# Norm stores moved to GpSimd's queue, and the first token half's transposed tiles copied to SBUF before they are split

## The chip, the cores and the metric

The kernel runs on one core of one Trainium2 chip. The metric is the device time of one execution in microseconds; lower is better. Before the change the median of three runs is 2728.11 us (2725.67, 2728.11 and 2728.45).

## What is computed

Two layers of a causal decoder on a sequence of 1024 tokens of width 1024, all in fp32. Layer 0 mixes tokens with dilated sliding-window attention, layer 1 with a gated linear recurrence (HGRN2). After each mixer comes a dense MLP, and every sub-layer ends in a layer norm:

```python
for i in range(DEPTH):                      # DEPTH = 2
    if i % 2 == 0:
        y = dilated_attention_mixer(x, attn_w_in[j], attn_w_out[j])
    else:
        y = hgrn2_mixer(x, hgrn_w_in[j], hgrn_w_out[j], hgrn_norm_g[j], lbs[i])
    x = layer_norm(ALPHA * x + y, ln_mix_g[i], ln_mix_b[i])
    y = jnp.square(jax.nn.relu(x @ ffn_w_up[i])) @ ffn_w_down[i]
    x = layer_norm(ALPHA * x + y, ln_ffn_g[i], ln_ffn_b[i])
```

The change touches the place, once per layer, where the mixer's output projection and its norm hand over to the MLP's up-projection.

## The kernel before, in words

**Numbers as pairs.** Every fp32 operand of a large matmul is split in two tiles: a high part (ScalarE copies it, rounded to `float32r`) and a low part (VectorE subtracts the high part from the source). A product is three matmuls: high by high, high by low, low by high. In the up-projection these are L1349, L1350 and L1351, of 128x128 weights by 512 columns; the low part of a weight tile `H` is needed first by L1351.

**Fast products.** The MLP uses a Strassen-like scheme with seven products on halves. The class `Fast` (L278 on) holds the normed input as transposed tiles: "11" and "21" for the first half of the tokens (tiles 0 to 3 of 128 tokens), "22" and "T1" to "T4" for the second half and for sums and differences of both.

**The norm stage, `outproj_ln` (L1062 on).** A closure `fin(t)` (L1187) finishes token tile `t`: the rows' remaining matmuls (L204 to L206) in one of three PSUM banks, the residual added by VectorE (L1199, L1201), the norm (`ln_math`, L214 on: statistics L228, scaling L230 and L244 on VectorE, small steps on ScalarE), and a store of 512 KB of the normed tile `z` to DRAM (L1204). The MLP's residual reads it back much later (L1516). `tr(t)` calls `Fast.add`, whose `z_tr` has TensorE transpose the tile (L253, four transposes to a bank) in the two PSUM banks of tag `pt`. In layer 0 the program's order is fin 0 to 3 with the column halves of tiles 5 and 6 in between, then tr 0, the rest of fin 6, tr 1, tr 2, the first half of fin 7, `weights()`, tr 3, fin 4, the second half of fin 7. `weights()` is the start of `ffn`: it asks for four 512 KB weight tiles `wa` (L1280) and splits the first three into `H` (L1310 on ScalarE, L1318 on VectorE). In layer 1 the order is similar, but fin 4 comes early and all of fin 7, both column halves, comes last.

**What `Fast.add` does with a tile of the first half.** `z_tr` leaves two banks `p0` and `p1`. For each of them `put` makes high and low parts in two steps of 256 columns (L263 on ScalarE, L264 on VectorE), both read from PSUM. Then both banks are copied whole to SBUF (`keep`, L321 and L322), for the sums of the second half. Only after that copy is a bank free for the next transposes. Tiles of the second half are transposed during the first up-products (`late`); GpSimd makes some of their differences (L328, L334).

**What sets the order.** All loads and stores touched here are issued by SyncE, whose queue (SPq) is in order: an issue that waits holds up those behind it. The instructions of an engine are put in an order when the program is built, by a planner that walks an estimated timeline, prefers what stands earlier in the program, and hands out buffers as it goes. Where the kernel wants an order of its own it pins it (`in_order`): for SyncE at the start of `outproj_ln`, and for TensorE, VectorE and SyncE from the seventeenth up-product on. The stage in between is left to the planner. Most SBUF tiles are slots of 4 KB per partition in one pool of 49 (`U`), and a slot is used again when its last reader, a store included, is done.

Of the kernel before, what the change touches and what calls it, by code (L numbers as in the profile page):

```python
# [12 lines left out]
AF = mybir.ActivationFunctionType  # L13
# [3 lines left out]
P = 128  # L17
# [52 lines left out]
def trunk_kernel(  # L70
# [24 lines left out]
    nc = tc.nc  # L95
# [10 lines left out]
    def bank(tag, name):  # L106
        return ps.tile([P, 512], F32, name=name, tag=tag, bufs={"mm": 3, "s": 2, "pt": 2, "o": 1}[tag])
# [4 lines left out]
    act = nc.scalar.activation  # L112
# [84 lines left out]
    def rows(ps_t, a, w, t, dm, ks, start, stop):  # L197

        n = len(ks)
        for i, k in enumerate(ks):  # L200
            ah, al = a[k]
            wh, wl = w[k][:2]
            c = slice(dm * 512, dm * 512 + 512)
            nc.tensor.matmul(ps_t, ah(t), wh[:, c], start=start and i == 0, stop=False)  # L204
            nc.tensor.matmul(ps_t, ah(t), wl[:, c], start=False, stop=False)
            nc.tensor.matmul(ps_t, al(t), wh[:, c], start=False, stop=stop and i == n - 1)  # L206
# [39 lines left out]
    def z_tr(z):  # L246

        out_ = []
        for j in range(2):
            pt = bank("pt", "lnpt")  # L250
            for i in range(4):
                k = j * 4 + i
                nc.tensor.transpose(pt[:, i * P:(i + 1) * P], z[:, k * P:(k + 1) * P], ident)  # L253
            out_.append(pt)
        return out_

    def put(his, los, src, c, eng=None):

        src = src.rearrange("p (k c) -> p k c", c=P)
        for i in range(2):  # L260
            hi = his[i].rearrange("p (k c) -> p k c", c=512)[:, :, c]
            lo = los[i].rearrange("p (k c) -> p k c", c=512)[:, :, c]
            act(hi, src[:, 2 * i:2 * i + 2], AF.Copy)  # L263
            (eng or nc.vector).tensor_sub(lo, src[:, 2 * i:2 * i + 2], hi.bitcast(F32))  # L264
# [13 lines left out]
    class Fast:  # L278
# [22 lines left out]
        def add(self, t, z):  # L301
            half, c = t // 4, slice((t % 4) * P, (t % 4) * P + P)
            first = not self.seen or self.seen[0] == half
            self.seen.append(half)
            v, g = nc.vector, nc.gpsimd
            p0, p1 = z_tr(z)

            def scratch(n):
                return wp.tile([P, 512], F32, name=f"fs{n}", tag="p" if n % 2 else "pts", bufs=3 if n % 2 else 4)

            def put_(n, src, eng=None):
                put(*self.tiles(n), src, c, eng)

            if half == 0:
                put_("11", p0)
                put_("21", p1)
            else:
                put_("22", p1)
            if first:
                a, b = ("11", "21") if half == 0 else ("12", "22")  # L320
                act(self.keep(a, t), p0, AF.Copy)  # L321
                act(self.keep(b, t), p1, AF.Copy)  # L322
                return
            t1, t2, t3, t4 = (scratch(n) for n in (1, 2, 3, 4))
            if half == 1:
                w12 = scratch(0)
                act(w12, p0, AF.Copy)
                g.tensor_sub(t1, w12, self.keep("11", t))  # L328
                v.tensor_sub(t3, p1, w12)
                v.tensor_sub(t2, p1, t1)  # L330
                yield
                put_("T2", t2)
                put_("T1", t1)
                g.tensor_sub(t4, self.keep("21", t), t2)  # L334
                yield
                put_("T3", t3)
                put_("T4", t4)
                return
            b22 = self.keep("22", t)
            v.tensor_sub(t1, self.keep("12", t), p0)  # L340
            g.tensor_sub(t3, b22, self.keep("12", t))
            g.tensor_sub(t2, b22, t1)
            put_("T1", t1)
            v.tensor_sub(t4, p1, t2)
            put_("T3", t3)
            yield
            put_("T2", t2)
            put_("T4", t4)
# [713 lines left out]
    def outproj_ln(pr, oN, fill, resid, gB_ap, bB_ap, keep, weights):  # L1062
# [15 lines left out]
        z = []  # L1078

        def load_z(t):  # L1080
            while len(z) <= min(t, 7):
                zt = U("z")
                nc.sync.dma_start(zt, resid(len(z)))
                z.append(zt)
# [102 lines left out]
        def fin(t, dms=(0, 1)):  # L1187
            load_z(t)
            for dm in dms:
                c = slice(dm * 512, dm * 512 + 512)  # L1190
                old = parts.get((t, dm), [])
                o = begun.pop((t, dm), None)
                fresh = o is not None or not old
                first = o is None
                if first:
                    o = bank("mm", "pmm")
                rows(o, a, w, t, dm, [k for k in range(NK) if k not in old], first, True)
                if fresh:
                    nc.vector.scalar_tensor_tensor(z[t][:, c], z[t][:, c], ALPHA, o, op0=ALU.mult, op1=ALU.add)  # L1199
                else:  # L1200
                    nc.vector.tensor_add(z[t][:, c], o, z[t][:, c])  # L1201
            if 1 in dms:
                ln_math(z[t], gB, bB, sums=pr.mixer == 0 and t in NSUM)
                nc.sync.dma_start(keep[t * P:(t + 1) * P, :], z[t])  # L1204

        if pr.mixer == 0:
            begin(5, 0, ks)
            begin(5, 1, ks, "s")
            fin(0)
            fin(5, (0,))  # L1210
            fin(1)
            fin(5, (1,))
            fin(2)
# [821 lines left out]
```

## Time and profile before

| | |
|---|---|
| median of 3 runs | 2728.11 us |
| the profiled execution | 2729.02 us, of which 2727.2 us is the span of the profile |
| granted TensorE clock, mean | 0.998 |
| the norm stage of layer 0, stores of `z` | from 1002.8 to 1040.5 us |
| the norm stage of layer 1, stores of `z` | from 2059.0 to 2110.9 us |
| issued by SyncE and ScalarE / by GpSimd | all DMAs / none |

How to read it: times in the trace count from the span's start. A busy TensorE is not TensorE at its peak: matmuls overlap, one of 512 columns is recorded with about 390 ns but the next starts about 227 ns after it. So the distance between starts tells a stall, and an idle time of zero does not rule one out.

### The profile page before, as it was taken

Reading aid. Unit: us, or ns where it says so; the run is one execution under the profiler, and the core shown is the slowest. Engines: PE = TensorE matmul, PEld = TensorE weight load, DVE = VectorE, ACT = ScalarE, POOL = GpSimd, SP = SyncE. Lnnn points to the kernel's source line nnn. Section 1 sums busy time; section 2 is a strip of 40 time slices with the busy share of each in tenths; the row PEclk is TensorE's granted clock in tenths of the full one; section 3 lists DMA queues with packets and bytes.
Section 4 is the critical chain, followed back from the end, with each engine's and each line's share of the span. In section 5 each row is a group of like instructions: output and inputs, shape, how many; then the busy total and the mean of one; then the engine's idle time right before and its main releaser. Section 6 shows DMA issues by size and latency. Waiting matters only on the chain.

```text
span 2727.2 us, 44137 instructions
## 1 busy us (share of the span) xinstructions
PE 2698.6 (99%) x16256; PEld 2199.0 (81%) x16256; DVE 2043.0 (75%) x3887; ACT 1387.0 (51%) x3044; POOL 28.3 (1%) x28
## 2 busy tenths in 40 slices
PE   9999999999999999999999999999999999999998
PEld 7787888888788677888888888788888888888887
DVE  8868877787787788776686686556578886678687
ACT  5555555555565456444554345556452544545443
POOL 0000000000000001000000000000000100000000
PEclk9999999999999999999999999999999999999999
DMA  7867666766867424553675652010242464485653
GB/s 297 273 225 236 210 219 204 239 224 213 257 209 237 126 105 171 186 200 137 220 253 180 221 170 93 32 62 32 74 128 110 150 224 166 152 305 176 221 177 127
DMA packets 208152, 493.66 MB, mean 181 GB/s; under 512 B 30016, under 2 KB 44864, under 8 KB 207936
## 3 DMA queue, kind: packets, MB, share of 16 engines
q1 hardware_dynamic: 206688, 489.53, 53.7%
q8 instruction: 128, 2.10, 0.3%
q10 hardware_dynamic: 1248, 1.31, 0.2%
q14 instruction: 88, 0.72, 0.1%
HBM read 362.69 MB, written 94.11 MB: 167 GB/s over the span
## 4 chain that ended last, share of the span: by engine, by line
PE 90%; DVE 6%; ACT 1%; DMA 1%; issue 1%; SPq 0%; DVEq 0%; ACTq 0%
PE pup L1351 7%; PE pup L1349 7%; PE pmm L828 7%; PE pup L1350 7%; PE pmm L826 7%; PE pmm L827 7%; PE pdy L1504 4%; PE pdy L1503 4%; PE pdy L1500 4%; PE pmm L192 3%; PE pdx L1503 3%; PE pdx L1504 3%; PE pdx L1500 3%; PE pmm L194 3%; PE pmm L193 3%; PE pmm L204 2%
## 5 line engine op out<-in xcount | busy, mean ns | idle before, releaser
L826 PE MATMUL pmm<-xh,H 128*128 128x512 f32 x1008 | 403.7, 400 | 1.6 <-ACT H L493 1.0
L828 PE MATMUL pmm<-xh,H 128*128 128x512 f32 x1008 | 395.0, 392 | 3.1 <-DVE H L501 2.9
L827 PE MATMUL pmm<-xl,H 128*128 128x512 f32 x1008 | 393.0, 390 | 0.9 <-DVE xl L158 0.9
L828 PEld LDWEIGHTS pmm<-xh,H 128*128 128x128 f32 x1008 | 189.2, 188 | 47.8 <-DVE H L501 6.9
L826 PEld LDWEIGHTS pmm<-xh,H 128*128 128x128 f32 x1008 | 189.5, 188 | 40.2 <-ACT H L493 1.9
L827 PEld LDWEIGHTS pmm<-xl,H 128*128 128x128 f32 x1008 | 189.7, 188 | 38.2 <-DVE xl L158 1.6
L1500 PE MATMUL pdy<-dT,dS 128*128 128x512 f32 x512 | 199.2, 389 | 0.0
L1503 PE MATMUL pdy<-dT,dS 128*128 128x512 f32 x512 | 199.2, 389 | 0.0
L1504 PE MATMUL pdy<-dT,dS 128*128 128x512 f32 x512 | 199.2, 389 | 0.0
L157 ACT ACTIVATE dS<-dr 128x512 fp32r<-128x512 f32 x192 | 119.4, 622 | 68.0 <-PE pdy L1504 36.2
L192 PE MATMUL pmm<-f0nh,wh 128*128 128x512 f32 x384 | 153.3, 399 | 0.0
L193 PE MATMUL pmm<-f0nl,wh 128*128 128x512 f32 x384 | 149.8, 390 | 0.0
L194 PE MATMUL pmm<-f0nh,wl 128*128 128x512 f32 x384 | 149.8, 390 | 0.0
L589 ACT ACTIVATE p<-p,stats 128x192 f32<-128x192 f32 (+1 forms) x256 | 108.9, 428 | 62.0 <-DVE stats L586 61.8
L158 DVE TENSOR_TENSOR dS<-dr,dS 128x512 fp32r<-128x512 f32 x192 | 130.9, 682 | 9.3 <-ACT dS L157 9.3
L157 ACT ACTIVATE dT<-hold 128x512 fp32r<-128x512 f32 x128 | 80.1, 625 | 80.3 <-DVE hold L1479 33.3
L1310 ACT ACTIVATE H<-wc 128x512 fp32r<-128x512 f32 x128 | 77.2, 625 | 78.4 <-DVE wc L1303 44.8
L1503 PEld LDWEIGHTS pdy<-dT,dS 128*128 128x128 f32 x512 | 96.1, 188 | 20.1
L1500 PEld LDWEIGHTS pdy<-dT,dS 128*128 128x128 f32 x512 | 96.1, 188 | 19.9
L1504 PEld LDWEIGHTS pdy<-dT,dS 128*128 128x128 f32 x512 | 96.1, 188 | 19.9
L586 DVE CUSTOM_DVE_ANT_0 p<-s,mask 128x192 f32<-128x192 f32 (+1 forms) x256 | 71.1, 337 | 45.6 <-PE s L573 32.6
L493 ACT ACTIVATE H<-wc 128x512 fp32r<-128x512 f32 x108 | 66.6, 629 | 75.3 <-DVE wc L485 73.3
(424 smaller groups left out, 6875.4 us busy)
## 6 DMA issues: line engine op xcount, KB each, us to landing
xh<-xtd SPq DMA_DIRECT2D x110, 512.0 KB
xl<-xtd SPq DMA_DIRECT2D x110, 512.0 KB
dr<-hd SPq DMA_DIRECT2D x192, 256.0 KB
dr<-in_w_down_dram SPq DMA_DIRECT2D x128, 256.0 KB
rot<-e SPq DMA_DIRECT2D x192, 128.0 KB
wa<-in_w_up_dram SPq DMA_DIRECT2D x48, 512.0 KB
wb<-in_w_attn_dram SPq DMA_DIRECT2D x36, 512.0 KB
wa<-in_w_attn_dram SPq DMA_DIRECT2D x33, 512.0 KB
```

What stands on the lines that cost most here:

```text
L157: act(hi, raw, AF.Copy)
L192: nc.tensor.matmul(o, wh[:, k], xs.h(k), start=k == 0, stop=False)
L193: nc.tensor.matmul(o, wh[:, k], xs.l(k), start=False, stop=False)
L194: nc.tensor.matmul(o, wl[:, k], xs.h(k), start=False, stop=k == NK - 1)
L826: nc.tensor.matmul(o, wh, hi[k // 2][:, c], start=begin and k == 0, stop=False, skip_group_check=True)
L827: nc.tensor.matmul(o, wh, lo[k // 2][:, c], start=False, stop=False, skip_group_check=True)
L828: nc.tensor.matmul(o, wl, hi[k // 2][:, c], start=False, stop=end and k == 3, skip_group_check=True)
L1349: nc.tensor.matmul(o, wh, xf.h(b, k), start=begin and k == 0, stop=False, skip_group_check=True)
L1350: nc.tensor.matmul(o, wh, xf.l(b, k), start=False, stop=False, skip_group_check=True)
L1500: nc.tensor.matmul(o[q], h, T_[:, L], start=begin, stop=False, skip_group_check=True)
L1503: nc.tensor.matmul(o[q], h, T_[:, R], start=False, stop=False, skip_group_check=True)
L1504: nc.tensor.matmul(o[q], l, T_[:, L], start=False, stop=end, skip_group_check=True)
```

## The change

Two edits. The first is in `Fast.add`: for a tile of the first half both banks are first copied whole to SBUF, and the four high and four low parts are then made from these copies and not from PSUM. The number of instructions and their sizes are the same. The second is in `fin`: the store of the normed tile is issued by GpSimd's queue instead of SyncE's. It applies to 16 stores, eight in each layer. The norms' stores inside `ffn` (L1536, L242) stay where they were.

```diff
@@ class Fast, add()
+            if first and half == 0:
+                for n, p in (("11", p0), ("21", p1)):
+                    act(self.keep(n, t), p, AF.Copy)
+                for n in ("11", "21"):
+                    put_(n, self.keep(n, t))
+                return
             if half == 0:
                 put_("11", p0)
                 put_("21", p1)
@@ outproj_ln, fin()
                 ln_math(z[t], gB, bB, sums=pr.mixer == 0 and t in NSUM)
-                nc.sync.dma_start(keep[t * P:(t + 1) * P, :], z[t])
+                nc.gpsimd.dma_start(keep[t * P:(t + 1) * P, :], z[t])
```

## The prediction

> **What bounds the kernel now.** I read the page first: busy times and the chain that ended last.
>
> ```profile
> span 2727.2 us, 44137 instructions
> PE 2698.6 (99%) x16256; PEld 2199.0 (81%) x16256; DVE 2043.0 (75%) x3887; ACT 1387.0 (51%) x3044; POOL 28.3 (1%) x28
> PE 90%; DVE 6%; ACT 1%; DMA 1%; issue 1%; SPq 0%; DVEq 0%; ACTq 0%
> ```
>
> TensorE sets the time. The change touches no matmul, so it can only win where TensorE stands still or runs at a lower clock, or lose by a new wait. Next, the busy times by stretches: the first five run through the hand-over of layer 0, the last lies in that of layer 1.
>
> ```profile
> 1030.00:1041.30 11.30, 8.30 (x29) 5.45 (x28) 10.32 (x20) 4.87 (x11) 1.27 (x1) 0.70 0.66 247
> 1041.30:1052.00 10.70, 10.70 (x52) 8.86 (x50) 7.48 (x11) 6.88 (x16) 3.10 (x2) 1.00 0.34 123
> 1052.00:1063.00 11.00, 9.64 (x44) 7.71 (x43) 10.92 (x24) 8.71 (x22) 2.81 (x1) 1.00 0.48 168
> 1063.00:1074.00 11.00, 11.00 (x55) 9.14 (x54) 8.90 (x18) 7.48 (x19) 2.65 (x2) 1.00 0.53 192
> 1074.00:1085.00 11.00, 10.91 (x52) 8.75 (x51) 11.00 (x21) 7.31 (x18) 3.61 (x2) 1.00 0.32 109
> 2090.00:2100.00 10.00, 10.00 (x51) 8.01 (x50) 7.15 (x15) 6.37 (x16) 0.00 (x0) 1.00 0.94 351
> ```
>
> Columns: length, then PE, PEld, DVE, ACT, POOL busy, the granted clock, DMA share, GB/s. Only 1030 to 1041.3 has a hole: TensorE is busy for 8.30 of 11.30 us, with a mean clock of 0.70, while VectorE is nearly full (10.32). The stretch of layer 1 has no hole and full clock: nothing is to be won there. TensorE in the hole, by its timeline:
>
> ```profile
> 1028.80 1.04 PE L253 MATMUL lnpt<-ident,z 128*128 128x128 f32 x8
> 1029.90 0.40 PE L206 MATMUL pmm<-woh,aol 128*128 128x512 f32 x1
> 1031.84 1.15 PE L253 MATMUL lnpt<-ident,z 128*128 128x128 f32 x8 [1.53 <-ACT af11r L321]
> 1033.18 0.85 PE L253 MATMUL lnpt<-ident,z 128*128 128x128 f32 x4 [0.20 <-ACT fs L327]
> 1033.70 0.80 PE L1349 MATMUL pup<-af11h,H 128*128 128x512 f32 x1
> 1037.40 0.80 PE L1351 MATMUL pup<-af11h,H 128*128 128x512 f32 x1 [1.26 <-DVE H L1318]
> 1038.00 0.63 PE L1349 MATMUL pup<-af11h,H 128*128 128x512 f32 x1
> 1038.43 0.63 PE L1350 MATMUL pup<-af11l,H 128*128 128x512 f32 x1
> 1040.46 0.40 PE L1349 MATMUL pup<-af11h,H 128*128 128x512 f32 x1
> 1040.69 0.39 PE L1350 MATMUL pup<-af11l,H 128*128 128x512 f32 x1
> 1041.38 0.39 PE L1349 MATMUL pup<-af11h,H 128*128 128x512 f32 x1
> ```
>
> The last row matmul ends at 1029.90 + 0.40 = 1030.30. Then TensorE waits 1.53 us for a bank that tile 3 still holds (L321 copies it to SBUF last), 0.20 us for the copy L327, and from 1033.70 for the up-projection's weights: it gets the first few matmuls done and stands until the low half of `H` is there (1037.40). Starts there are 0.43 us apart (1038.00 to 1038.43), from 1040.46 on 0.23: that is the half clock behind the 0.70. Without any of it, 12 transposes at 1.04/8 = 0.13 us at most and the 15 up-matmuls before 1041.38 at 0.23 us would end at 1030.30 + 1.56 + 3.45 = 1035.3. So **the hole is worth 6.1 us, and no more**.
>
> **The change part by part: stores.** SyncE's queue and the engines that feed the hole:
>
> ```profile
> 1002.77 23.93 SPq L1204 DMA_DIRECT2D x1d<-z  x6
> 1026.74 0.42 SPq L1083 DMA_DIRECT2D z<-in_x_dram  x1
> 1027.26 2.53 SPq L1280 DMA_DIRECT2D wa<-in_w_up_dram  x4
> 1032.82 8.03 SPq L1204 DMA_DIRECT2D x1d<-z  x2
> 1029.43 0.38 ACT L263 ACTIVATE af11h<-lnpt 128x256 fp32r<-128x256 f32 x1 [0.62 <-PE lnpt L253]
> 1031.18 0.60 ACT L321 ACTIVATE af11r<-lnpt 128x512 f32<-128x512 f32 x1
> 1031.68 0.59 ACT L322 ACTIVATE af21r<-lnpt 128x512 f32<-128x512 f32 x1
> 1032.53 0.60 ACT L327 ACTIVATE fs<-lnpt 128x512 f32<-128x512 f32 x1 [0.26 <-PE lnpt L253]
> 1033.02 0.62 ACT L1310 ACTIVATE H<-wa 128x512 fp32r<-128x512 f32 x1
> 1034.24 1.15 ACT L1310 ACTIVATE H<-wa 128x512 fp32r<-128x512 f32 x2 [0.59 <-DMA wa<-in_w_up_dram]
> 1031.52 1.27 DVE L244 SCALAR_TENSOR_TENSOR z<-z,lnw,bB 128x1024 f32<-128x1024 f32 x1
> 1033.91 1.28 DVE L228 BATCH_NORM_STATS2 lnst<-z 128x6 f32<-128x512 f32 x2
> 1035.46 1.28 DVE L230 SCALAR_TENSOR_TENSOR z<-z,lnmv,gB 128x1024 f32<-128x1024 f32 x1
> 1036.66 1.89 DVE L1318 TENSOR_TENSOR H<-wa,H 128x512 fp32r<-128x512 f32 x3
> 2114.80 0.73 ACT L263 ACTIVATE hfT2h<-fs 128x256 fp32r<-128x256 f32 x2
> ```
>
> Six stores stand ahead of the tile-7 load and the four weight loads on SyncE, and each waits for its norm: the weights are asked for at 1027.26 and the last split in this stretch still waits for one at 1034.24. Moved away, the stores hold up no load; the loads then go when their slots are free, at the earliest after the last issue before the stores and at the latest at 1027.26, so they gain between 0 and 24 us of lead (1026.74 - 1002.77). I take a few us, since the planner hands slots out in program order, behind those of tile 2's copies. On GpSimd's queue the same stores still wait for their norms. Behind them stand only L328 and L334:
>
> ```profile
> 1033.21 1.27 POOL L328 TENSOR_TENSOR fs<-fs,af11r 128x512 f32<-128x512 f32 x1 [939.20 <-ACT fs L327]
> 1047.94 1.67 POOL L334 TENSOR_TENSOR fs<-af21r,fs 128x512 f32<-128x512 f32 x1 [13.46 <-DVE fs L330]
> 1048.38 1.51 DVE L264 TENSOR_TENSOR afT2l<-fs,afT2h 128x256 fp32r<-128x256 f32 x1
> L264 DVE TENSOR_TENSOR af11l<-lnpt,af11h x8: 409/424/425, 1013.4 to 1030.7; 128x256 fp32r<-128x256 f32 x8
> L1516 SPq DMA_DIRECT2D z<-x1d x8: 319/350/424, 1444.4 to 1489.7; - x8
> ```
>
> Had the first L328 to wait for the last store (1032.82 + 8.03 = 1040.85), it would end at 1042.1 and still be ahead of the chain that takes it (13.46 us idle before L334). No row shows an issue by GpSimd: I bound it by SyncE's 2.53/4 = 0.63 us and GpSimd's own 1.67 us per instruction. 16 of them are 10 to 27 us on an engine that is busy for 28.3 of 2727.2 us; on TensorE's path I take 0, as the stored rows are first read at 1444.4 (L1516) and until then only the slots of `z` wait for a landing (rival 3).
>
> **Copies first.** Tile 3's first bank is full at 1029.43. Before, four split steps alternate between ScalarE and VectorE for 1031.18 - 1029.43 = 1.75 us and then come the copies. After, the copies run at 1029.43 and 0.50 us later (spacing of L321 and L322), so the banks are free at 1030.03 and 1030.53, when TensorE wants them at 1030.30 and 0.5 us later: **the 1.53 us wait goes**. The price: the splits end later. From SBUF, ScalarE's high parts follow each other without waiting for VectorE (2114.80: two in 0.73 us), so four take some 1.25 us behind the copies, to 1030.43 + 1.25 = 1031.7 instead of 1031.2. Next late is L327: behind the splits it runs 1031.7 to 1032.3 and not to 1033.13, so the third group of transposes still waits, and the first split of `H` ends at 1032.8 instead of 1033.65. Of the 1.53 us some 0.85 stay as gain at the first up-matmul.
>
> **The low half of `H`** ends last: 1037.40. VectorE has no idle time ahead of it; L1318 stands behind tile 7's statistics and scaling because the planner expected the weights late. With the loads ahead, and tile 2's and 3's copies 1.75 us earlier, it should expect them some 2 to 3 us earlier. Then L1318 goes ahead of L228, L229 and L230 and starts at about 1033.9 instead of 1036.66: 2.75 us. VectorE's splits of tile 3 start about 1 us later than now, which I charge with 0.55 us on that chain. So L1351 starts at 1037.40 - 2.75 + 0.55 = 1035.2.
>
> **The clock.** Here the half clock began in a pause of 1033.70 - 1030.30 = 3.40 us in which TensorE ran only transposes. That pause shrinks to about 2.5 us, and I take it that the clock stays full. From L1351 to 1041.38 are 11 matmuls; at 0.23 us they end at 1035.2 + 2.5 = 1037.7: **3.7 us gained**. With half clock as now (3.98 us from L1351 to 1041.38) it is 2.2 us; I take 3.7, since the pause is shorter than the only one that halved the clock here. [...]
>
> **Is it given back?** VectorE's idle time from 1041.3 to 1085 is 3.22 + 0.08 + 2.10 + 0 = 5.4 us, so it can follow 3.7 us, with little left; TensorE is full behind the hole, so the gain should last to the end.
>
> [...] Before, L264 reads one operand from PSUM; now both come from SBUF. Beside GpSimd's L334 a step with both from SBUF took 1.51 us (1048.38), those from PSUM at most 0.425 us. L328 at 1033.21 moves with L327 to about 1032.4 and the last splits end near 1032.1, so I take 0; caught, one step costs 1.51 - 0.42 = 1.1 us on VectorE's chain. [...]
>
> **Sum.** 2729.02 - 3.7 = 2725.3 for the profiled execution, which lies 0.9 us above the median: **2724.4 us**. Differences within 0.2% (5.5 us) can hardly be told from none.
>
> **The rivals.**
> (1) All of the hole goes: the loads, issued early, let the planner put L1310 and L1318 ahead of tile 3. For it: SyncE issues nothing but stores from 1002.77 to 1026.70, so the loads have 24 us to be early. Against: slots. 2728.11 - 6.1 = 2722.0.
> (2) VectorE holds it: L1318 stays behind tile 7's norm. For it: VectorE's chain has no gap from 1031.52 to 1036.66, and the splits of tile 3 come later. Then L1351 starts at 1037.4 to 1038.0, up to 1039.1 if GpSimd's read costs 1.1 us: nothing gained, up to 1.7 us lost. 2728 to 2730; also the case in which the change does not do what it says, since the bank was not what came last.
> (3) Slower: slots. Before tile 0 is transposed, 41 of 49 slots hold output weights, projections, seven `z` and the norm's factors; with twelve for the new tiles, eight freed, `z` 7, four `wa` and three `H` it is 53, so four of the last take over slots of `z` 0 to 3, whose stores now go another way. If a store is late by GpSimd's queue, `H` waits. For a loss of 5.5 us the first up-matmul must slip from 1033.70 to 1039.2, so tile 3's store, issued by 1026.7, must take 12 us to land. Against: 512 KB at the 247 GB/s of that stretch take 2.1 us. About 2734, the half clock included.
>
> **How the numbers follow.** Forecast 0.47, rival 1 0.18, rival 2 0.21, rival 3 0.14. Faster by over 0.2%: most of rival 1 and a quarter of the forecast, where the pause or L1318 comes out better, 0.28. Slower by over 0.2%: 0.13, rival 3. Within: 0.59. The range takes rival 1 less the 2.4 us by which the lowest run lies under the median, and reaches above rival 2 towards rival 3: 2719.6 to 2731.5.
>
> **What would show it.** In the profile after, the weights' issue moves ahead of 1027 and SyncE no longer waits on `z`; the wait on L321 is gone; L1318 starts near 1034; the clock of this stretch is near 1.00 and not 0.70; layer 1 is unchanged. If L1318 still starts at 1036 or later, rival 2 is right. If `H` or `wa` waits for a store's landing, rival 3. A new idle time of TensorE in layer 1 would make the whole sum wrong.

## The result and the profile after

The change makes the kernel a little faster: the median is 2723.65 us (20 executions, 2721.81 to 2725.72) against 2727.87 us before (20 executions, 2725.24 to 2729.61). The ratio is 0.9986, with a 95% interval of 0.9979 to 0.9992; that is 4.2 us, or 0.15%. The forecast was 2724.4 us. The profiled execution took 2721.81 us, of which 2720.0 us is its span.

The page after, with the span, the busy times and the chain that ended last:

```profile
span 2720.0 us, 44143 instructions
PE 2694.8 (99%) x16256; PEld 2199.3 (81%) x16256; DVE 2042.1 (75%) x3887; ACT 1385.0 (51%) x3044; POOL 39.2 (1%) x44
PE 92%; DVE 5%; ACT 1%; issue 1%; DMA 0%; POOL 0%; SPq 0%; DVEq 0%; ACTq 0%; POOLq 0%
```

GpSimd has 16 more instructions, the stores' issues, and is busy for 10.9 us more (39.2 against 28.3). VectorE's share of the chain falls from 6% to 5%. The same stretches as before, by windows (length, then PE, PEld, DVE, ACT, POOL busy, clock, DMA share, GB/s):

```profile
1030.00:1041.30 11.30, 11.30 (x56) 9.41 (x55) 11.17 (x22) 5.59 (x14) 2.80 (x3) 1.00 0.12 49
1041.30:1052.00 10.70, 7.78 (x42) 6.14 (x41) 10.70 (x21) 7.54 (x20) 4.55 (x3) 1.00 0.67 245
```

The hole is gone: from 1030 to 1041.3 TensorE is busy throughout and the clock is 1.00 instead of 0.70. But a new, smaller hole has opened behind it: in the next stretch TensorE is busy for 7.78 of 10.70 us, where it had been full before, and VectorE for 10.70 of 10.70 us, where it had 3.22 us to spare. TensorE by its timeline after:

```profile
996.45 0.39 PE L206 MATMUL pmm<-woh,aol 128*128 128x512 f32 x1
1028.27 0.39 PE L206 MATMUL pmm<-woh,aol 128*128 128x512 f32 x1
1028.50 0.39 PE L1355 MATMUL pup<-af11h,H 128*128 128x512 f32 x1
1033.94 1.04 PE L253 MATMUL lnpt<-ident,z 128*128 128x128 f32 x8
1037.59 0.39 PE L1355 MATMUL pup<-af21h,H 128*128 128x512 f32 x1
1046.21 0.50 PE L1357 MATMUL pup<-af11h,H 128*128 128x512 f32 x1 [1.68 <-DVE H L1324]
1050.45 0.63 PE L253 MATMUL lnpt<-ident,z 128*128 128x128 f32 x4 [1.24 <-DVE fs L336]
1104.35 0.39 PE L1355 MATMUL pup<-af22h,H 128*128 128x512 f32 x1
```

(Line numbers behind L311 are 6 higher after: L1318 is now L1324, L1349 to L1351 are L1355 to L1357.) The first up-matmul, 1028.50, follows the last row matmul, 1028.27, at full pace. Tile 3's transposes are done by then, and the first of the second half's tiles is transposed only at 1033.94, after two products. Then come the new stalls: 1.68 us for a low part of `H`, 1.24 us for a bank that VectorE's L336 still reads.

What this is worth is read from matmuls that both kernels have: the 261st row matmul (L204 to L206), the start of the fourth up-product and that of the 26th. Before, they stand here:

```profile
997.46 0.39 PE L206 MATMUL pmm<-woh,aol 128*128 128x512 f32 x1
1046.13 0.39 PE L1349 MATMUL pup<-af21h,H 128*128 128x512 f32 x1
1110.35 0.39 PE L1349 MATMUL pup<-af22h,H 128*128 128x512 f32 x1
```

From the first to the second it is 48.67 us before and 41.14 after: **7.5 us gained**. From the first to the third it is 112.89 and 107.90: 5.0 us are left. So 2.5 us were given back, 0.5 of them four transposes that the changed kernel makes only behind the fourth product. Between the fourth and the seventh product it loses 3.0 us: the two stalls above (2.9 us) and eleven transposes more in that stretch (16 against 5), less a stall of 1.36 us that the kernel before has there, at 1056.40. Where the weights' loads, the low parts of their splits and the neighbours stand after:

```profile
992.44 33.64 SPq L1286 DMA_DIRECT2D wa<-in_w_up_dram  x5
1025.84 1.89 DVE L1324 TENSOR_TENSOR H<-wa,H 128x512 fp32r<-128x512 f32 x3
1034.49 1.27 DVE L230 SCALAR_TENSOR_TENSOR z<-z,lnmv,gB 128x1024 f32<-128x1024 f32 x1
1041.60 1.67 POOL L340 TENSOR_TENSOR fs<-af21r,fs 128x512 f32<-128x512 f32 x1 [0.32 <-DVE fs L336]
1042.03 1.52 DVE L264 TENSOR_TENSOR afT2l<-fs,afT2h 128x256 fp32r<-128x256 f32 x1
1044.34 1.26 POOL L334 TENSOR_TENSOR fs<-fs,af11r 128x512 f32<-128x512 f32 x1 [1.08 <-DMA hd<-upa]
1044.41 1.75 DVE L1324 TENSOR_TENSOR H<-wa,H 128x512 fp32r<-128x512 f32 x1
```

The loads start at 992.44 and not at 1027.26; the low parts are made at 1025.84, ahead of tile 3 and of the last scaling of the stage (L230 at 1034.49), where before they stood behind it (1036.66 behind 1035.46). In the give-back two of VectorE's steps are stretched beside a subtraction of GpSimd: L264 takes 1.52 us, L1324 1.75, where the same steps without it take 0.41 (1047.69) and 0.68 (1047.09). The kernel before has the same pair (L264 for 1.51 us at 1048.38, and the row below), in a stretch where VectorE is busy for only 7.48 of 10.70 us. So the stretching is not new; the full VectorE around it is.

```profile
1049.82 1.78 DVE L1318 TENSOR_TENSOR H<-wa,H 128x512 fp32r<-128x512 f32 x1
```

The two spans differ by 7.2 us and the medians by 4.2. About 1.0 us of that lies ahead of the 261st row matmul, and 1.2 us around a wait for ScalarE near 1168 us (0.68 us of idle time at 1168.31), which the changed kernel's profile lacks. That is not the change's doing, since a second profile of the same kernel (`a2_again`) has it like the kernel before (0.63 us at 1163.69). In that second profile the gain up to the 26th product is again 5.0 us. A single pair of profiles is good to 1 or 2 us here, not better.

Part of the 7.5 us is the half clock, which the profile before has from 1033.50 to 1040.33 and the profile after has nowhere in this stage. The gain in the median is not that half clock alone. Of the executions measured together with `a2_again`, those of the kernel before with a mean clock of 0.999 have a median of 2727.55 us (11 executions), those of the changed kernel with 0.999 have 2723.41 us (9).

### The profile page after: what moved, and what is told of

It reads as the page before. It is cut to its first block, busy times and chain, and to the rows that moved or that the text cites. A ratio compares the mean times of both kernels' runs of the same rounds, so it can differ in the third digit from the quotient of the medians.

```text
span 2720.0 us, 44143 instructions
## 1 busy us (share of the span) xinstructions
PE 2694.8 (99%) x16256; PEld 2199.3 (81%) x16256; DVE 2042.1 (75%) x3887; ACT 1385.0 (51%) x3044; POOL 39.2 (1%) x44
## 4 chain that ended last, share of the span: by engine, by line
PE 92%; DVE 5%; ACT 1%; issue 1%; DMA 0%; POOL 0%; SPq 0%; DVEq 0%; ACTq 0%; POOLq 0%
PE pmm L834 7%; PE pmm L832 7%; PE pmm L833 7%; PE pup L1357 7%; PE pup L1355 7%; PE pup L1356 7%; PE pdy L1510 4%; PE pdy L1509 4%; PE pdy L1506 4%; PE pmm L192 3%; PE pdx L1509 3%; PE pdx L1510 3%; PE pdx L1506 3%; PE pmm L194 3%; PE pmm L193 3%; PE pmm L205 2%
```

## The experiments

The first theory was that both halves of the change are needed, early weights and an engine order that uses them. It fell with the second run. All results at a glance; "low part" is the start of the first L1318 (L1324) less that of the last scaling L230 of the stage, and the columns "4th" and "26th" say by how many us earlier than before these up-products start, counted from the 261st row matmul of the same profile. The column "half clock" says where in the profile between 990 and 1110 us the clock fell to one half, and for how long:

| kernel | median us | ratio, 95% interval | low part | 4th | 26th | half clock |
|---|---|---|---|---|---|---|
| before | 2727.87 | | +1.20 | 0 | 0 | 1033.50, 6.83 us |
| changed | 2723.65 | 0.9986 [0.9979, 0.9992] | -8.65 | 7.5 | 5.0 | none |
| `a2_again` | 2723.42 | 0.9984 [0.9976, 0.9993] | -8.66 | 7.6 | 5.0 | none |
| `e1_stores` | 2728.03 | 1.0004 [0.9995, 1.0013] | +1.20 | -0.3 | -0.3 | 1037.12, 3.41 us |
| `e2_copies` | 2724.02 | 0.9989 [0.9980, 0.9997] | -6.42 | 7.4 | 4.3 | 1047.47, 3.41 us |
| `e3_mark` | 2739.99 | 1.0045 [1.0033, 1.0058] | -10.22 | 1.2 | -10.9 | 1036.01, 3.41 us, and twice more |
| `c1_psum` | 2724.62 | 0.9990 [0.9981, 0.9999] | -2.77 | 2.5 | 2.4 | none |
| `d1_held` | 2723.84 | 0.9986 [0.9977, 0.9995] | -3.24 | 2.4 | 2.4 | 1033.43, 3.41 us |
| `g1_weights_up` | 2723.90 | 0.9987 [0.9978, 0.9996] | -11.88 | 5.5 | 3.7 | none |
| `f1_before_vsub` | 2722.86 | 0.9982 [0.9973, 0.9991] | -2.05 | 2.3 | 4.3 | none |
| `e6_low` | 2723.54 | 0.9987 [0.9978, 0.9996] | -8.66 | 7.5 | 3.7 | 1051.66, 3.41 us |
| `f2_vsub_low` | 2723.30 | 0.9981 [0.9972, 0.9990] | -8.66 | 7.5 | 4.6 | 1051.38, 3.41 us |
| `e5_vsub` | 2721.38 | 0.9978 [0.9969, 0.9986] | -8.66 | 7.5 | 6.9 | none |
| `f3_copies_vsub` | 2721.58 | 0.9977 [0.9968, 0.9987] | -5.31 | 7.4 | 6.8 | none |

### Which half of the change makes the gain

**The stores alone.** Against the kernel before:

```diff
-                nc.sync.dma_start(keep[t * P:(t + 1) * P, :], z[t])
+                nc.gpsimd.dma_start(keep[t * P:(t + 1) * P, :], z[t])
```

> Only the stores of the normed tiles go to GpSimd; the tiles of the first half are split from PSUM as before. Theory (the gain of 4.2 us needs two things at once: weights that are there early, and an order in which VectorE takes the splits of H ahead of tile 3 and tile 7): the order of TensorE, ScalarE and VectorE is that of before here, row for row, so L1318 still stands behind tile 7's scaling; the weights are asked for by about 1008 instead of 1027.26, only the 0.59 us wait of L1310 goes, the 1.53 us wait for L321 stays, and TensorE's first L1351 still comes at about 1037: 0 to 0.8 us gained, ratio 0.9997 to 1.000. Rival A (the early weights alone make the gain): first L1351 by about 1034, the whole 4.2 us, ratio 0.9985. Rival S (what is measured is scatter of the runs): no stall of the trace changes.

Measured: 2728.03 us against 2727.64 in the same runs, so no gain. SyncE, VectorE and TensorE by the timeline:

```profile
992.38 33.41 SPq L1280 DMA_DIRECT2D wa<-in_w_up_dram  x5
1034.45 1.28 DVE L230 SCALAR_TENSOR_TENSOR z<-z,lnmv,gB 128x1024 f32<-128x1024 f32 x1
1035.65 1.89 DVE L1318 TENSOR_TENSOR H<-wa,H 128x512 fp32r<-128x512 f32 x3
1030.82 1.14 PE L253 MATMUL lnpt<-ident,z 128*128 128x128 f32 x8 [1.53 <-ACT af11r L321]
1036.39 0.50 PE L1351 MATMUL pup<-af11h,H 128*128 128x512 f32 x1 [2.46 <-DVE H L1318]
```

The weights are asked for 35 us earlier than before, and nothing comes of it. The order of TensorE, ScalarE and VectorE is that of the kernel before, row for row from 991 to 1109 us, so L1318 stands behind the scaling as before. The bank wait is the same 1.53 us. What TensorE saves ahead of L1351, by earlier high parts and by a clock that falls only at 1037.12, it spends waiting for the low parts: 2.46 us instead of 1.26.

**The copies alone.** The changed kernel, with the store back on SyncE (the diff above, reversed).

> Only the copies go first; the stores stay on SyncE. Theory (both needed): the engines' order is nearly that of the changed kernel (the three L1324 stand ahead of tile 7's L229, behind tile 3's splits), but the weights are still asked for at about 1027 and land at 1030 to 1034; L1324 now waits for them and what is queued behind it on VectorE (tile 7's norm, tile 4's scaling) waits too. First L1357 at about 1033 to 1035 instead of 1037.4 before and 1029 after: 1 to 3 us gained, ratio 0.9989 to 0.9996, and SyncE waits for z as before. Rival B (the banks and the order make it, the loads were never late): as the changed kernel, 4.2 us, ratio 0.9985. Rival A (the loads alone make it): nothing, ratio 1.000.

Measured: 2724.02 us, 3.6 better than before and not to be told from the whole change. SyncE and VectorE by the timeline:

```profile
1013.55 0.74 SPq L1286 DMA_DIRECT2D wa<-in_w_up_dram  x1
1022.12 0.38 SPq L1286 DMA_DIRECT2D wa<-in_w_up_dram  x1
1025.88 1.22 SPq L1286 DMA_DIRECT2D wa<-in_w_up_dram  x2
1030.10 2.99 DVE L1324 TENSOR_TENSOR H<-wa,H 128x512 fp32r<-128x512 f32 x3
```

The theory was wrong about the loads, and rival B has the number. The loads do not stay behind the six stores: with the copies first the planner puts them between the stores, and the first two, which hold all that the first three splits need, are asked for at 1013.55 and 1022.12. So the copies bring about both, a new order and earlier loads. The high parts are done at 1027.44 without a wait; the low parts come at 1030.10, directly behind a residual addition of VectorE, and that is early enough: at the fourth product this kernel is 7.4 us ahead, the whole change 7.5.

**The changed kernel once more**, to see which stalls come back.

> The changed kernel once more, for what differs from run to run. Median 2723.0 to 2724.5 us. Theory (the new stalls are a matter of the order of VectorE): the stalls of L1357 near 1046 (1.85 us), of the transposes near 1050 (1.24 us) and of L1355 near 1062 (0.63 us) are there again to 0.3 us. Rival (they come of chance meetings of VectorE with GpSimd's reads): they come out different by more than half, or at other places.

They come back to within 0.02 us (idle times of 1.69, 1.23 and 0.48 us, at 1047.20, 1051.44 and 1063.45, against 1.68, 1.24 and 0.47), so they belong to the order of the work and not to chance.

**The stores moved, but SyncE still waiting.**

```diff
                 nc.gpsimd.dma_start(keep[t * P:(t + 1) * P, :], z[t])
+                nc.sync.dma_start(mark_d[pr.mixer, t], z[t][:, 0:1])
```

> The changed kernel with one thing added: beside each store on GpSimd SyncE writes one column of the same normed tile (512 bytes) to a scratch place in memory, at the place in the program where the store stood. The 512 KB still go by GpSimd, but SyncE waits for each norm again and holds up the loads behind it. Theory (what the stores did was to hold up the loads): as with the copies alone, 1 to 3 us better than before, ratio 0.9989 to 0.9996, the weights asked for near 1027. Rival Q (what matters is that 512 KB leave by another queue, for instance because they no longer compete with the loads): as the changed kernel, ratio 0.9985.

Measured: 12 us slower than before, outside what either theory expected. The profile shows why this says little on the question. The landing times of GpSimd's 16 stores, in the changed kernel and here, and TensorE here:

```profile
DMA to landing us min/median/max: 2.9/3.1/6.5
```
```profile
DMA to landing us min/median/max: 9.7/11.3/18.6
```
```profile
1035.22 0.50 PE L1357 MATMUL pup<-af11h,H 128*128 128x512 f32 x1 [4.15 <-ACT H L1318]
```

The added column is 128 pieces of 4 bytes, and beside it the 512 KB stores land later, after 11.3 us in the median and not 3.1. So do the weights: the first two tiles are asked for at 1015.21 and 1023.74, but their splits begin only at 1034.54 and 1037.58, after idle times of 7.0 and 2.4 us on ScalarE, and TensorE waits 4.15 us. That the small pieces are the reason was not tested. The run shows that late weights do cost time in this order, but not what SyncE's waits alone cost.

### Banks, loads or order

**Copies first, but splits from PSUM.** Against the copies alone:

```diff
-                for n in ("11", "21"):
-                    put_(n, self.keep(n, t))
+                for n, p in (("11", p0), ("21", p1)):
+                    put_(n, p)
```

> As the copies alone (stores on SyncE, both banks copied whole first), but the four high and four low parts are then made from PSUM as before and not from the copies, so that a bank stays taken until its last split. Theory after the first four runs (the gain comes from the banks being free early, which lets the planner put the rest of the stage in another order): the copies' place alone does nothing, the weights are asked for behind the six stores again, L1324 stands behind tile 7's scaling: 2726.5 to 2728.5 us, ratio 0.9996 to 1.0003. Rival O (it is enough that the copies stand first): as the copies alone, 2724.0, ratio 0.9988.

Measured: 2724.62 us, 3.2 better than before. The theory expected nothing, so it fell too. TensorE and VectorE:

```profile
1030.76 1.09 PE L253 MATMUL lnpt<-ident,z 128*128 128x128 f32 x8 [1.42 <-DVE af11l L264]
1035.15 0.50 PE L1357 MATMUL pup<-af11h,H 128*128 128x512 f32 x1 [1.28 <-DVE H L1324]
1034.42 1.88 DVE L1324 TENSOR_TENSOR H<-wa,H 128x512 fp32r<-128x512 f32 x3
1037.19 1.29 DVE L230 SCALAR_TENSOR_TENSOR z<-z,lnmv,gB 128x1024 f32<-128x1024 f32 x1
```

The bank is held as long as before (1.42 us of waiting), yet there is a gain: L1324 now stands ahead of the last scaling. Counted from the 261st row matmul the first low-part matmul comes 1.2 us earlier (1035.15 - 996.38 = 38.77 against 1037.40 - 997.46 = 39.94), and the remaining 1.3 of the 2.5 us are the half clock, which does not come.

**Copies first, loads held back.** Against the copies alone, in layer 0:

```diff
                     nc.sync.dma_start(raw[k], w_up[li, p + half * NP])
+                    if n < 4 and not last:
+                        behind(latest(), stored[-1:])
```

> As the copies alone, but in layer 0 the first four weight loads are held on SyncE behind the sixth store, where they stood before. TensorE's order is then that of the copies alone to within a few rows. Theory L (with the banks free early the weights' lead is still needed, and the loads between the stores gave it): the weights are asked for at 1025 to 1026, the last of the first three lands at about 1032, the low parts L1328 come at 1033 to 1035 and the up-projection stands 2 to 4 us: ratio 0.9994 to 0.9999. Rival N (the order alone does it, the lead is worth nothing): as the copies alone, ratio 0.9988.

Measured: 2723.84 us. SyncE and VectorE (line numbers are shifted by the edit: L1328 and L231 are L1324 and L230):

```profile
1024.33 2.21 SPq L1288 DMA_DIRECT2D wa<-in_w_up_dram  x4
1032.18 1.88 DVE L1328 TENSOR_TENSOR H<-wa,H 128x512 fp32r<-128x512 f32 x3
1035.42 1.28 DVE L231 SCALAR_TENSOR_TENSOR z<-z,lnmv,gB 128x1024 f32<-128x1024 f32 x1
```

TensorE by its timeline, at the first low-part matmul:

```profile
1032.91 0.50 PE L1361 MATMUL pup<-af11h,H 128*128 128x512 f32 x1 [1.08 <-DVE H L1328]
```

Theory L was right about the place: at the fourth product this kernel is only 2.4 us ahead, the copies alone 7.4. Of the 5.0 us between them 1.6 are a half clock, which this profile has from 1033.43 on: from the first low-part matmul to the fourth product it takes 9.02 us, and `c1_psum`, at full clock, 7.43. Another 0.5 are four transposes that stand ahead of the fourth product here and behind it there. The remaining 2.9 are put down to the lead of the loads. At the 26th product it is still 2.4 against 4.3, partly because the copies alone get a half clock later, from 1047.47, and the medians cannot be told apart: what the lead brings in the hole is mostly lost again behind it.

**Neither copies first nor banks freed.** The stores alone, with the call of `weights()` moved up:

```diff
+            weights()
             tr(2)
             fin(7, (0,))
-            weights()
             tr(3)
```

> Stores on GpSimd and, in place of the copies first, the call that asks for and splits the first weights moved up in the program in front of the transposes of tile 2 (layer 0); the first half's tiles are split from PSUM as before. VectorE's order then differs from that of before in a few rows: the three L1318 stand about 16 rows earlier. Theory (what the copies did was to bring the splits of H forward in VectorE's order; the banks matter less): the wait for L321 stays at about 1.5 us, the low parts of H are there before the first up-product wants them, no half clock; 2 to 4 us gained, ratio 0.9985 to 0.9993. Rival B (without the banks free early there is no gain): 2727 to 2728.5, ratio 0.9997 to 1.0004.

Measured: 2723.90 us; the order theory's number. Beside `e1_stores` the program differs by the place of one call, and that is 4 us (ratios 0.9987 and 1.0004). It has no half clock in this stage, where `e1_stores` has one of 3.41 us. VectorE and TensorE:

```profile
1025.77 1.89 DVE L1318 TENSOR_TENSOR H<-wa,H 128x512 fp32r<-128x512 f32 x3
1029.55 1.14 PE L253 MATMUL lnpt<-ident,z 128*128 128x128 f32 x8 [0.59 <-ACT af11r L321]
```

The bank wait is shorter here than expected, 0.59 us and not 1.5, but it is there.

### What was given back

**Low parts directly behind high ones**, in the changed kernel:

```diff
             split_up(n + SPLITUP)
+            if n < NAHEAD:
+                low_up()
```

> The changed kernel, in which for the first eight up-products the low part of H (L1324) follows its high part in the program instead of standing one product later. TensorE's order is the same, row for row. Theory (the 1.85 us at 1046 are lost because L1324 stands behind the late tiles' work on VectorE): that stall goes, and with it some of the 3.0 us that the changed kernel loses from 1043 to 1051; 1.5 to 2.5 us better than the changed kernel, about 2721.5, ratio 0.9976 to 0.9980. Rival (VectorE has no room there: what stood ahead of it becomes late instead): the transposes near 1050 wait the longer, ratio 0.9983 to 0.9986.

Measured: 2723.54 us, no better than the change: the rival's case. TensorE:

```profile
1050.97 0.63 PE L253 MATMUL lnpt<-ident,z 128*128 128x128 f32 x4 [3.64 <-DVE fs L336]
```

The 1.68 us stall is gone, and the transposes that had waited 1.24 us now wait 3.64. Behind that wait the clock halves for 3.41 us: from the seventh product to the eighth the lead over the kernel before falls from 4.1 to 2.5 us, where the changed kernel keeps its 4.6. VectorE has no room, busy for 13.97 of 14 us from 1041 to 1055: what is moved ahead makes something else late.

**GpSimd's differences on VectorE**, in the changed kernel:

```diff
-                g.tensor_sub(t1, w12, self.keep("11", t))
+                v.tensor_sub(t1, w12, self.keep("11", t))
-                g.tensor_sub(t4, self.keep("21", t), t2)
+                v.tensor_sub(t4, self.keep("21", t), t2)
```

> The changed kernel, with the two differences that GpSimd makes for a late tile (L334, L340) given to VectorE; GpSimd then only issues stores in this stage. Theory (the loss from 1043 to 1051 comes of VectorE's steps being stretched beside GpSimd's reads: L264 1.52 instead of 0.41 us, L1324 1.75 instead of 0.68): no step of VectorE from 1036 to 1062 takes more than 1.3 us, the stalls at 1046 and 1050 shrink by half or more, 1 to 2 us better than the changed kernel, ratio 0.9978 to 0.9982. Rival (VectorE is short of time and the eight differences at 0.68 us weigh more than the stretching): same or slower than the changed kernel, ratio 0.9985 or more.

Measured: 2721.38 us, ratio 0.9978; 2.0 to 2.3 us under the two medians of the changed kernel, though the intervals still overlap. VectorE and TensorE:

```profile
1041.25 0.68 DVE L1324 TENSOR_TENSOR H<-wa,H 128x512 fp32r<-128x512 f32 x1
1048.92 0.50 PE L1355 MATMUL pup<-af21h,H 128*128 128x512 f32 x1 [1.52 <-ACT upa L1360]
```

As the theory said: the step that took 1.75 us takes 0.68, VectorE makes the subtractions as well and is done earlier, and of the 3.0 us lost between the fourth and seventh product 1.3 remain. The largest stall left, of 1.52 us, waits for ScalarE. Beside GpSimd's subtractions L264 and L1324 took 1.52 and 1.75 us in the changed kernel; without them, here, they take 0.42 (at 1041.85) and 0.68.

**The same edit on the kernel before.**

> The kernel before, with the late tiles' two differences on VectorE instead of GpSimd; nothing else. Theory (VectorE's stretched steps beside GpSimd's reads cost nothing there, because VectorE still had idle time behind the hole; only the change used it up): 2727 to 2728.5, ratio 0.9997 to 1.0004. Rival (the stretching costs time in any kernel, so that the gain of 2 us is apart from the change): 2725.5 to 2726, ratio 0.9990 to 0.9994.

Measured: 2722.86 us, 5 us better. Theory and rival were both wrong, since the edit does more than move work: it changes the order of VectorE. VectorE by its timeline:

```profile
1033.92 1.89 DVE L1318 TENSOR_TENSOR H<-wa,H 128x512 fp32r<-128x512 f32 x3
1035.97 1.28 DVE L230 SCALAR_TENSOR_TENSOR z<-z,lnmv,gB 128x1024 f32<-128x1024 f32 x1
```

Again L1318 has come ahead of the scaling. So the 2 us of `e5_vsub` cannot be put down to the stretching alone; the order of the steps behind the hole changed there as well, and that was not separated.

**Both**, and **without the stores' move** (the copies alone, with the two subtractions on VectorE):

> The changed kernel with the differences on VectorE and the low parts of H directly behind the high ones, both together. Theory (with VectorE relieved the largest stall left, 1.69 us near 1049, waits for ScalarE's L1360 and not for a low part): as with the differences alone, 2721.4, ratio 0.9976 to 0.9980. Rival (late low parts hold up the products still, through the banks that wait for them): 0.5 to 1.5 us better than with the differences alone, ratio 0.9972 to 0.9975.

> Copies first and differences on VectorE, with the stores left on SyncE. Theory (the stores' part of the change is worth nothing once the copies stand first, as the loads then go out between the stores): 2721 to 2722.3, ratio 0.9976 to 0.9981. Rival (the stores' part was worth 1 us or more and VectorE's lack of time hid it): 2722.5 to 2723.5, ratio 0.9982 to 0.9986.

Measured: 2723.30 us with the low parts ahead as well, 1.9 us worse than with the differences alone, so neither theory's number: the low parts push the transposes back here too (2.0 us of waiting for L336), and behind that wait comes a half clock, over which the lead falls from 5.0 us at the seventh product to 3.4 at the eighth. Without the stores' move it is 2721.58 us, as with it (2721.38), which is what the theory had. `e5_vsub` and `f3_copies_vsub` both lie about 2 us under the changed kernel, with intervals that overlap its own; the stores' move adds nothing that can be measured.

**Where this leaves the theories.** Leaving `e3_mark` aside, whose L1318 (there L1326) stands ahead too but whose weights come late, the kernels divide cleanly by one row: where L1318 stands behind the last scaling of the stage (before, `e1_stores`) the time is 2728, where it stands ahead of it the time is 2721 to 2725, whichever edit put it there. `e1_stores` and `g1_weights_up` show the order as a cause: the stores' move without a new order brings nothing, and with one call moved it brings 4 us. That it is this one row fits TensorE's waits for L1318, but it is not shown by itself, since the planner moved other rows with it (in `g1_weights_up` 16 transposes stand between the last row matmul and the fourth product, before 12). How far ahead hardly matters for the total, which fits a VectorE that is full behind the hole. Why the planner lays out a new order when the copies stand first, or when a subtraction changes its engine, was not tested.

## Why the prediction came out right in sum and not in its steps

**The bound.** The hole was the right place, and its size was right. From the last row matmul to the fourth product it is 16.23 us before (1046.13 - 1029.90) and 9.32 after (1037.59 - 1028.27); four transposes fewer lie in between, about 0.5 us, so 6.4 us went, where 6.1 had been worked out as all there was. The rest of the 7.5 us lies ahead of the hole, so "no more" than 6.1 was too strict.

**The stores.** This step failed. "Moved away, the stores hold up no load", and "with the loads ahead" the planner "should expect them some 2 to 3 us earlier": the loads did go early, by 35 us where the prediction had allowed for 24 at most, and in `e1_stores`, with the same lead, the order stayed as it was. The copies changed the order, and took the loads forward with it.

**The bank wait.** It went, as forecast, but it was not what decided: `c1_psum` keeps 1.42 us of it and gains 3.2 us.

**The low half of H.** The step "L1318 goes ahead of L228, L229 and L230" was right in kind. `c1_psum` is nearly the case that was forecast: the low parts ahead of the scaling, no half clock, 2.5 us against the 3.7 of the sum. The changed kernel went further, ahead of tile 3 as in rival 1, which had been given 0.18 because of the slots; no slot held it up.

**The half clock.** It vanished, but the reason given ("the pause is shorter than the only one that halved the clock here") does not hold: `f1_before_vsub` keeps the full clock through a pause of 3.39 us, and `d1_held` loses it where no wait is longer than 1.08 (see the last section).

**Given back.** "The gain should last to the end" failed: of 7.5 us at the fourth product 5.0 remained. The 5.4 us of idle time in VectorE were counted for the whole of 1041 to 1085, but the need was in the first 10 us, where it had 3.22. The stretching beside GpSimd's subtractions, costed at 0 because it would not meet the splits of tile 3, met the steps behind them (1.52 and 1.75 us). It had done so in the kernel before (1.51 and 1.78 us), but there VectorE had idle time to take it up.

So the hole was undersized by 3.8 us (7.5 against 3.7) and the give-back by 2.5, and the two errors nearly cancel. That the number came out was luck: the hole closed as in rival 1, not as in the forecast, and the give-back that brought it back to the forecast was put at nothing. Rival 2 did not come for the whole change, though `e1_stores` is its case: L1318 stays behind the scaling and nothing is gained. Rival 3 did not come either: no split waited for a store, which landed within 6.5 us where 12 would have been needed. Layer 1 did not move: from the end of layer 0's up-projection to that of layer 1's, the changed kernel's lead over the kernel before stays the same to 0.3 us.

## What to carry to other kernels

Loads that come earlier gain nothing as long as the engine that uses them takes that work late in its order (in `e1_stores` they come 35 us earlier, and the time is 2728.03 us); look first at what stands ahead of the late instruction on its own engine. An edit that looks local, such as the place of a copy, can act through the order that a planner makes of everything around it, so compare the order of the instructions before explaining a gain by the edit's purpose, and the clock of two profiles before putting a price on their difference. And a hole closed on one engine is worth only what the next busiest engine can follow in the next few microseconds: here 5.0 of 7.5 us stayed, with VectorE busy for all of the 10.70 us behind the hole.

## What the runs showed of the hardware

**The half clock follows no single length of pause.** Before, the clock fell from 1.00 to 0.50 at 1033.50, towards the end of 3.40 us in which TensorE ran only transposes. `f1_before_vsub` has the same pause, from 1028.13 + 0.40 to 1031.92, and keeps a clock of 1.00 throughout. `e2_copies` loses the clock in a pause of 2.23 us, while the changed kernel keeps it at the same place in one of 1.68. `d1_held` loses it where the longest wait is the 1.08 us shown above. The rows of `f1_before_vsub` and the pause of `e2_copies`:

```profile
1028.13 0.40 PE L206 MATMUL pmm<-woh,aol 128*128 128x512 f32 x1
1031.92 0.50 PE L1349 MATMUL pup<-af11h,H 128*128 128x512 f32 x1
```
```profile
1047.69 0.80 PE L1357 MATMUL pup<-af11h,H 128*128 128x512 f32 x1 [2.23 <-DVE H L1324]
```

TensorE's work just ahead gives no limit in these rows either. The 3.41 us that end with a fall (length, TensorE busy, clock, DMA share, GB/s), of the kernel before, `e2_copies` and `d1_held`, with the half clock behind the last:

```profile
1030.09:1033.50 3.41, 1.68 (x12) 1.00 1.01 387
1044.06:1047.47 3.41, 1.40 (x11) 1.00 0.51 179
1030.02:1033.43 3.41, 1.93 (x6) 1.00 0.64 261
1033.43:1036.84 3.41, 3.41 (x9) 0.50 0.16 62
```

Then two stretches of the same length with no fall behind them, one with most of the pause of `f1_before_vsub` and one with the 1.68 us of the changed kernel:

```profile
1029.20:1032.61 3.41, 2.35 (x14) 1.00 1.02 394
1044.01:1047.42 3.41, 1.73 (x8) 1.00 0.67 207
```

The changed kernel keeps the clock with 1.73 us of work in its stretch, and `d1_held` loses it with 1.93. `f1_before_vsub` has 12 transposes and two other matmuls in its stretch, `d1_held` six matmuls and no transpose. What sets the moment of a fall these rows do not show.

**A store issued by GpSimd** costs that engine 0.53 to 0.70 us and lands 2.9 to 6.5 us after its issue in the changed kernel's first profile. Neither was on the path: the chain that ended last has 0% of POOL, POOLq and DMA.
